# Transposes between the halves of a tile's product, two tiles later, and other banks for the prologue's transposes

## The chip, the core and the metric

The kernel runs on one core of a Trainium2 chip. The core has TensorE (PE; its weight loads, PEld, overlap its matmuls), VectorE (DVE), ScalarE (ACT), GpSimd (POOL) and SyncE (SP), which issues the transfers. Each engine works through its own instructions in order and waits on semaphores for the others. PE writes into PSUM, which has eight banks of 128 x 512 float32 values. The metric is the device time of one execution in microseconds; the kernel before takes 1225.94 us (median of three runs, 1224.2 to 1227.89).

## What is computed

One layer of an encoder over 1024 tokens with 1024 features: a mixer (a gated linear recurrence beside latent attention) and a convolutional GLU network, each behind a normalisation and with a residual.

```python
h = x
h = h + hybrid_mixer(rms_norm(h, ln_mix_g), ...)   # two groups, each normalised, then y @ w_o
h = h + conv_glu_ffn(rms_norm(h, ln_ffn_g), w_up, ffn_conv_w, ffn_conv_b, w_down)
return rms_norm(h, final_norm_g)

def conv_glu_ffn(xn, w_up, ffn_conv_w, ffn_conv_b, w_down):
    u = xn @ w_up
    u = depthwise_conv(u, ffn_conv_w, ffn_conv_b, FFN_CONV_LEFT)
    return (jax.nn.silu(u[..., :D_FF]) * u[..., D_FF:]) @ w_down
```

## The kernel before

**Number format.** Matmul operands are kept as a high and a low part. `split` (lines 60 to 67) writes the high part with a copy (L62, ACT as a rule) and the low part with a subtraction (L67, on DVE or GpSimd). A product takes three matmuls, high by high, high by low and low by high (L70 to L72 in `mm3`, L1076 in `prod`).

**Stage A, the loop over eight token tiles (L1021 to L1045).** For tile i, in the order of the source: `mla_in(i + 1)` transposes the attention part of the next tile into a PSUM tile `psyt` and splits it into `yl` (high on ACT, low on DVE). `mix` then makes the product of tile i with the output weights in two column halves of twelve matmuls, `pso{i}0b` and `pso{i}1b`, and after each half DVE adds it to the residual `hh[i]` (L930). The tile is stored to `hs` by SP (L1026). `tr2` transposes the scaled tile of one tile earlier on PE (L942) and splits it into the operand forms of the next stage: two forms (`B11`, `B21`) for tiles 0 to 3, one (`B22`) for tiles 4 to 7. `norm2(i)` squares the tile on ACT (L935), works out the root on small columns and scales the tile in place on DVE (L937). GpSimd makes sums and differences of tiles in place (`sums_a`, `sums_b`, L955 to L961), and parts of the first weights are split in between.

All PSUM tiles of this loop come from `oneC`, a pool with four buffers of one bank: psyt, two halves, and one tile for each form of `tr2`.

**Stage B, the prologue of the up-projection (L1084 to L1125).** The product with `w_up` is made by a seven-product scheme for 2 x 2 blocks. Its operand forms are `B11`, `B21`, `B22` and the sums `T1` to `T4`; `tr_sum(f, j)` transposes a quarter of one and splits it (ACT, then DVE). `prod(n, j, bank)` is twelve matmuls. The transposes use PSUM banks that no product needs yet: `spare` takes the next of the list `spares` in turn, and banks are taken off the list before products claim them. The first weights are split here too (`W[0, 1]`, its low part on DVE).

**Order.** Both stages stand in one block in which PE, ACT, DVE, GpSimd and SP each keep the order of the source. A second such block begins behind the transposes of `T4`, with `prod(7, 0)` and `prod(3, 0)`. The two blocks are not tied to each other, so instructions of the second may be put ahead of the first one's last. From the second column pair of weights on, the kernel is a regular stream of products, and then the down-projection.

The lines on which the order of banks rests:

```python
def oneC(name):
    return psC.tile([P, 512], F32, tag="one", bufs=4, name=name)

turn, spares = [0], [VH[0], VH[1], GH, T1, S1]

def spare(name):
    turn[0] += 1
    return spares[turn[0] % len(spares)]
```

Of the kernel before, what the change touches and what calls it, by code (L numbers as in the profile page):

```python
# [20 lines left out]
NT = S // P  # L21
# [19 lines left out]
def encoder_layer(ctx, tc, x, w_in, wq, wk, wv, gw, wo, wup, wdn, vec, g_mix, g_ffn, g_fin, g_q, g_kv, tab_t, tab_n, out):  # L41
    nc = tc.nc
    act, dve, pool, pe = nc.scalar, nc.vector, nc.gpsimd, nc.tensor
# [675 lines left out]
    with ExitStack() as apx2:  # L719
# [112 lines left out]
        for t in range(2, NS - 3):  # L832
            h, i = divmod(t, NT)
# [43 lines left out]
        r1 = rsqrt(ssq[:, 0:NT + 2], NT + 2, 1.0 / 512, "r1")  # L877
# [22 lines left out]
    with sbpool("op", side="right") as op:  # L900
# [18 lines left out]
        def halves(ps):  # L919
            return [ps[:, 0:512], ps[:, 512:1024]]  # L920

        def mix(ps, yl, grp, i=None, rr=None):
            for n in range(2):
                mix_mm(ps[n], yl, grp, n)
                if rr is not None:
                    add_to_h(i, ps, rr, (n,))

        def add_to_h(i, ps, rr, parts=(0, 1)):
            for n in parts:
                dve.scalar_tensor_tensor(out=hh[i][:, ts(n, 512)], in0=ps[n], scalar=rr, in1=hh[i][:, ts(n, 512)], op0=ALU.mult, op1=ALU.add)  # L930
# [15 lines left out]
        def tr2(i, one):  # L946
            if i < 4:
                to_form("B11", i, hh[i][:, 0:512], one)
                to_form("B21", i, hh[i][:, 512:1024], one)
            else:  # L950
                to_form("B22", i, hh[i][:, 512:1024], one)
# [6 lines left out]
        def sums_b(i, eng):  # L958
            a, c = hh[i - 4], hh[i]
            eng.tensor_tensor(out=c[:, 512:1024], in0=c[:, 512:1024], in1=a[:, 0:512], op=ALU.subtract)  # L960
            eng.tensor_tensor(out=a[:, 512:1024], in0=a[:, 512:1024], in1=c[:, 512:1024], op=ALU.subtract)  # L961

        def tr_sum(f, j, one):
            src = {"T1": hh[j][:, 0:512], "T2": hh[j + 4][:, 512:1024], "T3": hh[j + 4][:, 0:512], "T4": hh[j][:, 512:1024]}[f]
            to_form(f, j, src, one)
# [24 lines left out]
        yls = {2: yle[2], 3: lru_in(3)}  # L990
        acc = {0: halves(early[0]), 1: halves(early[1])}
        load_wo(4, st4, wo345[:, 1], False)
        for i in range(2, NT):
# [9 lines left out]
            if i == 3:  # L1003
# [3 lines left out]
                r2 = rsqrt(ssq[:, NT + 2:2 * NT], NT - 2, 1.0 / 512, "r2")  # L1007
# [13 lines left out]
        for i in range(NT):  # L1021
            if i + 1 < NT:
                yls[i + 1] = mla_in(i + 1, oneC(f"psyt{i + 1}"))
            acc[i] = [oneC(f"pso{i}{n}b") for n in range(2)]
            mix(acc[i], yls[i], 1, i, r1[:, NT + i:NT + i + 1] if i < 2 else r2[:, i - 2:i - 1])
            nc.sync.dma_start(out=hs[i], in_=hh[i])  # L1026
            if i >= 1:
                tr2(i - 1, oneC)
            norm2(i)
            if i >= 5:  # L1030
                sums_b(i - 1, pool)
            if 4 <= i < NT - 1:
                sums_a(i, pool)
            if i == 0:
                fetch(0)
            if i == 1:
                split(W[0, 0][:, 0], W[0, 0][:, 1], raw[0][0], "act", "pool")
            if i == 2:
                s3 = stp.tile([P, 4, P], F32, tag="st", name="s30")
                combine(0, s3, pool)  # L1040
            if i in (3, 4):
                W[i - 2, 0] = wp.tile([P, 2, NK, P], F32R, tag="w", name=f"w{i - 2}0")
                split(W[i - 2, 0][:, 0], W[i - 2, 0][:, 1], raw[0][i - 3], "act", "pool")
            if i == 5:
                W[3, 0] = wp.tile([P, 2, 4, P], F32R, tag="w", name="w30")  # L1045
                split(W[3, 0][:, 0], W[3, 0][:, 1], s3, "act", "pool")
                fetch(1)
# [8 lines left out]
        S1, T1 = bank("S", "s1"), bank("T", "t0")  # L1056
        VL, VH = [None, None], [None, None]
        for j in range(2):
            VL[j], VH[j] = bank(f"L{j}", f"vl{j}"), bank(f"H{j}", f"vh{j}")
        GL, GH = bank("GL", "gl0"), bank("GH", "gh0")  # L1060
        turn, spares = [0], [VH[0], VH[1], GH, T1, S1]
# [9 lines left out]
    def prod(n, j, ps, new):  # L1071
        z, ko, f = PRODUCTS[n]
        w, b = W[z, j], B[f]
        for k in range(4):
            for l, r, a_, z_ in ((0, 0, new and k == 0, False), (0, 1, False, False), (1, 0, False, k == 3)):
                pe.matmul(ps, w[:, l, ko + k, :], b[:, r, k, :], start=a_, stop=z_, skip_group_check=True)  # L1076
# [6 lines left out]

    W[0, 1] = wo345[:, 1].rearrange("p z (k n) -> p z k n", k=NK)  # L1084
    c0 = stp.tile([P, S], F32, tag="st", name="c0")
    tr_sum("T2", 0, spare)
    prod(1, 0, VL[0], True)
    sums_a(7, dve)
    tr_sum("T2", 1, spare)
    tr_sum("T2", 2, spare)  # L1090
    split(W[0, 1][:, 0], W[0, 1][:, 1], raw[1][0], "act", "dve")
    copy(c0[:, lo], VL[0])
    prod(2, 0, GL, True)
    tr2(7, spare)
    sums_b(7, dve)
    add(GL, GL, c0[:, lo])
# [15 lines left out]
    copy(C11[1], S1)  # L1112
    add(C11[1], VL[1], C11[1])
    prod(6, 0, VL[0], False)
    tr_sum("T1", 3, spare)
    for j in range(3):
        tr_sum("T3", j, spare)
    copy(c0[:, hi], VL[0])
    spares.remove(T1)
    prod(5, 0, T1, True)  # L1120
    tr_sum("T3", 3, spare)
    for j in range(4):
        tr_sum("T4", j, spare)
# [207 lines left out]
    for j in range(1, NPAIR):  # L1331
# [20 lines left out]
        if j == 1:  # L1352
            GH = bank("GH", f"gh{j}")
# [3 lines left out]
        if j > 1:  # L1357
            prod(6, j, vl, False)
            GH = bank("GH", f"gh{j}")
# [56 lines left out]
    for n, (p, q) in enumerate(todo[:-LAST]):  # L1416
# [10 lines left out]
        acc = ys if p in (1, 3, 5) else xs  # L1427
# [99 lines left out]
```

## Time and profile before

| | |
|---|---|
| median of three runs | 1225.94 us (1224.2 to 1227.89) |
| the profiled execution | 1227.5 us, of which the span is 1225.7 us |
| PE busy | 1167.1 us, 95% of the span |
| DVE, ACT, GpSimd busy | 939.6 us (77%), 641.3 us (52%), 260.2 us (21%) |
| chain that ended last | PE 81%, DVE 12%, ACT 2%, DMA 2%, issue 2% |
| mean granted clock of PE | 0.987 of full speed |

Stage A's loop over tiles lies from 504 to 562 us of the span, stage B from 562 to 597 us, and the regular stream begins near 625 us. The granted clock has two levels, 1.2 and 2.4 GHz; a value between 0.5 and 1 for a stretch says which part of it ran at the lower one. In the timeline a row gives the start, the duration, the engine and line, the operation, what it writes and reads with the shapes, and in brackets the idle time of the engine just before it and what ended that.

### The profile page before, as it was taken

Reading aid. Unit: us, or ns where it says so; the run is one execution under the profiler, and the core shown is the slowest. Engines: PE = TensorE matmul, PEld = TensorE weight load, DVE = VectorE, ACT = ScalarE, POOL = GpSimd, SP = SyncE. Lnnn points to the kernel's source line nnn. Section 1 sums busy time; section 2 is a strip of 40 time slices with the busy share of each in tenths; the row PEclk is TensorE's granted clock in tenths of the full one; section 3 lists DMA queues with packets and bytes.
Section 4 is the critical chain, followed back from the end, with each engine's and each line's share of the span. In section 5 each row is a group of like instructions: output and inputs, shape, how many; then the busy total and the mean of one; then the engine's idle time right before and its main releaser. Section 6 shows DMA issues by size and latency. Waiting matters only on the chain.

```text
span 1225.7 us, 15357 instructions
## 1 busy us (share of the span) xinstructions
PE 1167.1 (95%) x5668; PEld 970.8 (79%) x5668; DVE 939.6 (77%) x1386; ACT 641.3 (52%) x1037; POOL 260.2 (21%) x146
## 2 busy tenths in 40 slices
PE   5999986999999999998899999999999999999997
PEld 5987764788888888776778888888888888888885
DVE  5788789877777765478697778787787877887866
ACT  4735565776767764343554445444444454344453
POOL 2214556621212243254010101101010100000000
PEclk8999998999999999999999999999999999999999
DMA  5311101000000133221233232322333258853333
GB/s 211 96 43 44 43 18 35 18 1 1 1 1 1 35 138 121 68 88 51 60 121 107 77 116 96 120 95 78 112 112 121 80 178 304 288 173 119 96 112 120
DMA packets 93579, 113.38 MB, mean 92 GB/s; under 512 B 5184, under 2 KB 59840, under 8 KB 93504
## 3 DMA queue, kind: packets, MB, share of 16 engines
q1 hardware_dynamic: 93504, 112.40, 27.8%
q8 instruction: 44, 0.72, 0.3%
q14 instruction: 31, 0.25, 0.1%
HBM read 82.76 MB, written 28.57 MB: 91 GB/s over the span
## 4 chain that ended last, share of the span: by engine, by line
PE 81%; DVE 12%; ACT 2%; DMA 2%; issue 2%; SPq 0%; DVEq 0%; POOL 0%; ACTq 0%
PE vl L1076 19%; PE x L1269 9%; PE y L1269 7%; PE gh L1076 5%; PE gl L1076 4%; PE pt L763 4%; PE p L1076 4%; PE av L774 3%; PE av L773 2%; PE sc L70 2%; PE sc L71 2%; PE sc L72 2%; DVE bc L223 1%; PE pso L71 1%; PE pso L72 1%
## 5 line engine op out<-in xcount | busy, mean ns | idle before, releaser
L1076 PE MATMUL vl<-T,w 128*128 128x512 f32 x792 | 195.7, 396 | 2.0 <-ACT gl L1082 1.5
L1076 PEld LDWEIGHTS vl<-T,w 128*128 128x128 f32 x792 | 148.5, 188 | 37.8 <-ACT gl L1082 1.9
L67 POOL TENSOR_TENSOR w<-rg,w 128x1024 fp32r<-128x1024 f32 x21 | 52.0, 2475 | 363.8 <-ACT w L62 227.6
L749 DVE TENSOR_REDUCE nm<-sc 128x1 f32<-128x1024 f32 x64 | 78.1, 1221 | 29.9 <-PE sc L72 29.6
L62 ACT ACTIVATE ptb<-pt 128x512 fp32r<-128x512 f32 x128 | 70.2, 596 | 58.3 <-PE pt L763 57.1
L67 DVE TENSOR_TENSOR ptb<-pt,ptb 128x512 fp32r<-128x512 f32 x128 | 83.0, 680 | 7.0 <-ACT ptb L62 7.0
L756 ACT ACTIVATE pr<-sc,nm 128x1024 f32<-128x1024 f32 x64 | 71.7, 1120 | 2.6 <-DVE nm L749 2.6
L763 PE MATMUL pt<-ident,pr 128*128 128x128 f32 x512 | 67.7, 274 | 3.3 <-DVE ptb L67 3.3
L763 PEld LDWEIGHTS pt<-ident,pr 128*128 128x128 f32 x512 | 59.3, 140 | 14.1 <-DVE ptb L67 5.3
L1076 PE MATMUL gh<-B,w 128*128 128x512 f32 x264 | 64.3, 392 | 1.4 <-DVE T L67 1.4
L773 PE MATMUL av<-ptb,vt 128*128 128x256 f32 x256 | 64.9, 292 | 0.0
L1173 ACT ACTIVATE c<-gh,vv 128x512 f32<-128x512 f32 x22 | 17.1, 778 | 89.1 <-DVE gh L1079 89.1
L774 PE MATMUL av<-ptb,vt 128*128 128x256 f32 x256 | 62.6, 283 | 0.0
L1076 PE MATMUL p<-T,w 128*128 128x512 f32 x252 | 62.5, 397 | 0.0
L1269 PE MATMUL x<-abS 128*128 128x512 f32 x264 | 60.2, 389 | 0.0
L1269 PE MATMUL y<-abS 128*128 128x512 f32 x264 | 60.2, 389 | 0.0
L1076 PEld LDWEIGHTS gh<-B,w 128*128 128x128 f32 x264 | 49.5, 188 | 13.0 <-DVE T L67 1.7
L1076 PE MATMUL vl<-B,w 128*128 128x512 f32 x240 | 58.4, 392 | 0.0
L1269 PEld LDWEIGHTS x<-abS 128*128 128x128 f32 x264 | 49.5, 188 | 10.3
L1269 PEld LDWEIGHTS y<-abS 128*128 128x128 f32 x264 | 49.5, 188 | 10.3
L1076 PE MATMUL gl<-B,w 128*128 128x512 f32 x240 | 57.6, 389 | 0.0
L1076 PEld LDWEIGHTS p<-T,w 128*128 128x128 f32 x252 | 47.4, 188 | 11.4
(647 smaller groups left out, 2972.8 us busy)
## 6 DMA issues: line engine op xcount, KB each, us to landing
rg<-in_wup SPq DMA_DIRECT2D x22, 512.0 KB, 4.2
rv<-in_wup SPq DMA_DIRECT2D x22, 512.0 KB, 3.8
S<-c SPq DMA_DIRECT2D x44, 256.0 KB, 2.6
wr<-in_wdn SPq DMA_DIRECT2D x44, 256.0 KB, 5.0
stS<-S SPq DMA_DIRECT2D x44, 256.0 KB, 2.9
A<-c SPq DMA_DIRECT2D x33, 256.0 KB, 2.1
stA<-A SPq DMA_DIRECT2D x33, 256.0 KB, 4.5
wost<-in_wo SPq DMA_DIRECT2D x8, 512.0 KB, 3.8
```

The lines of the kernel that those rows point to most:

```text
L62: act.activation(hi, src, AF.Copy)
L67: (dve if lo_on == "dve" else pool).tensor_tensor(out=lo, in0=src, in1=hi.bitcast(F32), op=ALU.subtract)
L70: pe.matmul(ps, l[0], r[0], start=start, stop=False)
L71: pe.matmul(ps, l[0], r[1], start=False, stop=False)
L72: pe.matmul(ps, l[1], r[0], start=False, stop=stop)
L749: dve.reduce_max(nm[t], sc[t], axis=AX, negate=True)
L756: act.activation(pr[t], sc[t], AF.Exp, bias=nm[t], accum_out=rowsum[:, h, i:i + 1])
L763: pe.transpose(pt[:, ts(c, P)], pr[t][:, ts(4 * kh + c, P)], ident)
L773: pe.matmul(av[:, 0:256], lv, ptb[buf][:, 0, c, :], start=(c == 0), stop=False)
L774: pe.matmul(av[:, 0:256], lv, ptb[buf][:, 1, c, :], start=False, stop=(c == NT - 1))
L1076: pe.matmul(ps, w[:, l, ko + k, :], b[:, r, k, :], start=a_, stop=z_, skip_group_check=True)
L1269: pe.matmul(ps, ab[:, 0, l, ts(j, P)], ab[:, 1, r, :], start=a_, stop=z_, skip_group_check=True)
```

## The change

`mix` takes a function and calls it between its two column halves. In the loop, `tr2` runs there, for the tile two earlier (i - 2) where it ran behind both halves for the tile one earlier. `sums_b` follows one iteration later. `tr2(6)` and `sums_b(6)` move behind the loop, to the start of stage B. In stage B the third quarter of `T2` is transposed behind `prod(2, 0)`, so that its split comes behind the split of the weight `W[0, 1]`. From `prod(6)` on the list of banks is set by hand: the transposes ahead of `prod(5)` leave out its bank `T1`, and the last four use the banks `VH`, not `GH`, which `prod(3)` writes next.

```diff
@@ -919,11 +919,13 @@
-        def mix(ps, yl, grp, i=None, rr=None):
+        def mix(ps, yl, grp, i=None, rr=None, between=None):
             for n in range(2):
                 mix_mm(ps[n], yl, grp, n)
                 if rr is not None:
                     add_to_h(i, ps, rr, (n,))
+                if n == 0 and between is not None:
+                    between()
@@ -1022,13 +1024,12 @@
             if i + 1 < NT:
                 yls[i + 1] = mla_in(i + 1, oneC(f"psyt{i + 1}"))
             acc[i] = [oneC(f"pso{i}{n}b") for n in range(2)]
-            mix(acc[i], yls[i], 1, i, r1[:, NT + i:NT + i + 1] if i < 2 else r2[:, i - 2:i - 1])
+            mix(acc[i], yls[i], 1, i, r1[:, NT + i:NT + i + 1] if i < 2 else r2[:, i - 2:i - 1],
+                (lambda: tr2(i - 2, oneC)) if i >= 2 else None)
             nc.sync.dma_start(out=hs[i], in_=hh[i])
-            if i >= 1:
-                tr2(i - 1, oneC)
             norm2(i)
-            if i >= 5:
-                sums_b(i - 1, pool)
+            if i >= 6:
+                sums_b(i - 2, pool)
             if 4 <= i < NT - 1:
                 sums_a(i, pool)
@@ -1083,14 +1084,16 @@
     c0 = stp.tile([P, S], F32, tag="st", name="c0")
+    tr2(6, spare)
+    sums_b(6, pool)
     tr_sum("T2", 0, spare)
     prod(1, 0, VL[0], True)
     sums_a(7, dve)
     tr_sum("T2", 1, spare)
-    tr_sum("T2", 2, spare)
     split(W[0, 1][:, 0], W[0, 1][:, 1], raw[1][0], "act", "dve")
     copy(c0[:, lo], VL[0])
     prod(2, 0, GL, True)
+    tr_sum("T2", 2, spare)
     tr2(7, spare)
     sums_b(7, dve)
@@ -1112,12 +1115,14 @@
     prod(6, 0, VL[0], False)
+    spares[:] = [VH[0], VH[1], GH]
     tr_sum("T1", 3, spare)
     for j in range(3):
         tr_sum("T3", j, spare)
     copy(c0[:, hi], VL[0])
-    spares.remove(T1)
     prod(5, 0, T1, True)
+    spares[:] = [GH, VH[0], VH[1], VH[0], VH[1]]
+    turn[0] = -1
     tr_sum("T3", 3, spare)
     for j in range(4):
         tr_sum("T4", j, spare)
```

## Rows read from the trace of the kernel before

**Rows 1.** Waits, 505 to 630 us: engine, line, waited for: total us, times, longest

```profile
PE pshB L942 <- DVE h L937: 3.8, 3, 1.6
PE vl L1076 <- DVE wo L67: 2.6, 1, 2.6
PE gh L1076 <- DVE T L67: 1.4, 1, 1.4
PE t L1076 <- DVE T L67: 1.3, 1, 1.3
```

**Rows 2.** Timeline of iterations 1 and 2, the forms, psyt, stores and scaling

```profile
515.78 0.68 DVE L67 TENSOR_TENSOR yl<-psyt,yl 128x512 fp32r<-128x512 f32 x1
...
516.52 0.42 PEld L942 LDWEIGHTS pshB<-ident,h 128*128 128x128 f32 x4 [0.18 <-DVE yl L67]
...
517.18 0.42 PEld L915 LDWEIGHTS psyt<-ident,yn 128*128 128x128 f32 x4 [0.24 <-DVE h L930]
...
522.85 2.21 DVE L937 SCALAR_TENSOR_TENSOR h<-h,rh1r,g 128x1024 f32<-128x1024 f32 x1 [2.78 <-DMA hs<-h]
524.98 0.68 DVE L67 TENSOR_TENSOR yl<-psyt,yl 128x512 fp32r<-128x512 f32 x1
```

**Rows 3.** Timeline of PE in iteration 4, to the start of iteration 5

```profile
533.54 0.60 PE L915 MATMUL psyt<-ident,yn 128*128 128x128 f32 x4
...
536.75 0.39 PE L70 MATMUL pso41b<-wo,yl 128*128 128x512 f32 x1
...
540.35 0.60 PE L915 MATMUL psyt<-ident,yn 128*128 128x128 f32 x4
```

**Rows 4.** Timeline of ACT, DVE and GpSimd in the same iteration

```profile
534.28 1.06 ACT L935 ACTIVATE jk<-h 128x1024 f32<-128x1024 f32 x1
...
536.57 1.28 DVE L937 SCALAR_TENSOR_TENSOR h<-h,rh3r,g 128x1024 f32<-128x1024 f32 x1
...
536.78 3.32 POOL L67 TENSOR_TENSOR w<-rg,w 128x1024 fp32r<-128x1024 f32 x1 [7.86 <-ACT w L62]
...
537.77 0.68 DVE L67 TENSOR_TENSOR yl<-psyt,yl 128x512 fp32r<-128x512 f32 x1
...
539.67 0.75 DVE L930 SCALAR_TENSOR_TENSOR h<-pso41b,r2r,h 128x512 f32<-128x512 f32 x1 [0.56 <-PE pso41b L72]
```

**Rows 5.** The tile hs: its eight stores, issue to landing

```profile
DMA to landing us min/median/max: 2.6/2.8/4.9
```

**Rows 6.** Timeline of PE: two matmul groups behind waits

```profile
200.64 0.50 PE L70 MATMUL psq<-cT,wq1h 128*128 128x512 f32 x1 [3.56 <-POOL wq1h L66]
...
572.35 3.85 PE L1076 MATMUL vl<-B,wo 128*128 128x512 f32 x10 [2.58 <-DVE wo L67]
```

**Rows 7.** Stretches: us, PE, PEld, DVE, ACT, POOL busy (x), PEclk, DMA, GB/s

```profile
200.00:205.00 5.00, 4.36 (x12) 3.36 (x13) 3.86 (x4) 2.44 (x3) 4.62 (x4) 0.66 0.01 3
...
524.00:529.00 5.00, 3.70 (x20) 2.86 (x21) 4.74 (x10) 3.07 (x6) 4.71 (x3) 1.00 0.24 97
...
570.00:575.00 5.00, 2.65 (x8) 2.13 (x9) 4.79 (x7) 0.00 (x0) 0.00 (x0) 0.83 0.01 3
```

**Rows 8.** Timeline of DVE and GpSimd near 551 us; the page's group of GpSimd splits

```profile
551.32 2.20 DVE L937 SCALAR_TENSOR_TENSOR h<-h,rh5r,g 128x1024 f32<-128x1024 f32 x1
...
551.15 1.29 POOL L961 TENSOR_TENSOR h<-h,h 128x512 f32<-128x512 f32 x1
...
L67 POOL TENSOR_TENSOR w<-rg,w 128x1024 fp32r<-128x1024 f32 x21 | 52.0, 2475 | 363.8 <-ACT w L62 227.6
```

**Rows 9.** Timeline: the loop's end (PE, DVE) and the prologue's end (PE)

```profile
559.53 0.39 PE L72 MATMUL pso71b<-wo,yl 128*128 128x512 f32 x1
...
561.80 0.73 DVE L930 SCALAR_TENSOR_TENSOR h<-pso71b,r2r,h 128x512 f32<-128x512 f32 x1
...
594.90 0.60 PE L942 MATMUL gh<-ident,h 128*128 128x128 f32 x4
...
608.79 3.07 PE L1076 MATMUL vl<-T,w 128*128 128x512 f32 x12 [0.47 <-ACT gh L1082]
```

## The prediction

> **What bounds the kernel now.** I read the page first: TensorE (PE) is busy 95% of the span and carries 81% of the chain that ended last, so time can only be won where PE waits. The list of waits from 505 to 630 us was next: in the stretch that the change touches, PE waits 3.8 us for the scaled token tiles (three times), 2.6 us for the low half of a weight split, 1.4 and 1.3 us for PSUM banks that VectorE (DVE) has yet to read [rows 1]. That is 9.1 us, about all the change could remove on PE directly. Then I read the stretch in order of time, because the edit moves work inside a loop that uses only four PSUM banks. Everything behind 625 us is a regular PE stream; a shift of its start is a shift of the end.
>
> **The loop over tiles: who holds which bank.** Each iteration takes five banks in this order: one for the attention transposes of the next tile (psyt), two for the halves of the product, two for the two forms of `tr2`. There are four buffers, so the second form must get the bank of this iteration's psyt, and that bank is free only when DVE has written the low split `yl` of the next tile. The trace shows just that: in iteration 1 the second group of form transposes loads when `yl` has ended (515.78 + 0.68 = 516.46; load at 516.52), and the next psyt loads when a half's add (DVE h L930) has ended, the bank's holder by the same turn [rows 2]. Before the change this costs 0.2 us, since the forms come after both halves. The edit puts them after the first half, 2.7 us earlier in PE's order, and the second half queues behind them.
>
> DVE can't give that bank sooner. Its order is the order of the source: the `yl` split stands behind the scaling of the tile before (L937), and that scaling overwrites the tile which the store `hs` is still reading, so it waits for the store [rows 2]. The new cycle, from the start of one second half to the next, is worked out from these rows: half to its add 2.92 us (536.75 to 539.67), the add 0.75, the store 2.75 (2.6 to 2.8 but for the early ones), the scaling 1.2 until `yl` can start (536.57 to 537.77), `yl` 0.68, four transposes 0.44 and about 0.1 of handover: 8.85 us. PE's own cycle today is 540.35 - 533.54 = 6.8 us [rows 2 to 5]. So PE, which ran through iterations 3 and 4 without a gap, would wait 2.0 us in each of iterations 3, 4 and 5.
>
> **Iteration 2 is worse.** Its second form waits for `yl` of tile 3, which ends at 524.98 + 0.68 = 525.66 in both kernels: it hangs on a slow early store, for which the scaling of tile 1 stands 2.8 us until 522.85, and on 2.21 us of scaling [rows 2], neither touched. PE would have reached it near 519.7, so it stands 6.0 us, in place of 1.6 us now. Second half of tile 2: from 526.2.
>
> **The clock.** After PE idled 3.56 us before 200.64, and 2.58 us before 572.35, the granted clock of the next stretches was 0.66 and 0.83 of full speed, which is a fall from 2.4 to 1.2 GHz for part of them; the ten matmuls at 572.35 took 3.85 us, where 0.23 us apart would give 2.3 [rows 6, 7]. So I put 1.5 us on each wait of 2.6 us or more, and none on waits of 2.0 us (after the 1.6 us wait ahead of 525.2 the clock stayed at 1.00 [rows 7]).
>
> **GpSimd and DVE.** In iteration 3 GpSimd splits a weight (L67) 2.5 us after the square of the tile starts (534.28 to 536.78). Today DVE's scaling began 0.2 us before it, and GpSimd's split took 3.32 us, where such splits take 2.48 on the mean [rows 4, 8]. In the other order DVE pays: the scaling at 551.32 began behind GpSimd's 551.15 and took 2.20 in place of 1.28 [rows 4, 8]. With the forms gone from between, the square starts at once behind the add, so GpSimd is ready 2.5 us after the add, the scaling 2.75 us after it. GpSimd is ahead by 0.2 us, so I take it that the scaling waits out the split: 2.0 us once. PE's wait there becomes 3.4 to 4.0 us, and another 1.5 us of clock follows. The bounds for this term are 0 and 3.5 us.
>
> The Trainium skill, SBUF — State Buffer, "Who interferes with whom", says that a DVE instruction with two SBUF inputs and a GpSimd instruction that reads SBUF exclude each other, and that whoever issues first holds the shared ports for the whole instruction. The two rows above agree with it in both orders. By the rule the term is either the full 2.0 us or nothing, not a share of it.
>
> **Sum of the loop.** From 526.2: +1.5 (clock) and three cycles of 8.85, +2.0 and +1.5 for iteration 3's collision, bring the second half of tile 5 to 557.8; it ends at 560.5. Iterations 6 and 7 have one form each and no such wait: 7.0 (psyt 0.36, 0.6 until the last add frees a bank, halves 2.84 and 2.72, a form 0.44) and 6.0. The last half ends at 573.5, against 559.53 + 0.23 = 559.8 now [rows 9]: **13.7 us later**, or 10.2 without the collision. The waits at 553 and 560 (2.2 us) are gone in that sum already.
>
> **From the loop's end to the matmul that waits for the weight.** Today that is 572.35 - 559.8 = 12.6 us [rows 6, 9]. The wait is for the low split of `W[0, 1]`, fifth in DVE's line behind the last scaling. The edit takes one form's split from ahead of it (T2 of tile 6) and puts another there (B22 of tile 6, by `tr2(6)`): the same count, 0.6 off and 0.6 on. What can be won is DVE's lag: its last add of the loop starts at 561.80, 1.8 us after it could read the half [rows 9]; in the new loop DVE is late by the scaling of tile 6 alone. I take -0.5 us (bounds -1.7 and +0.5), and leave the clock's fall there as it is.
>
> **Banks in the prologue.** After `prod(6)`, T1's bank is left out of the turn: `prod(5)` no longer waits 1.3 us for its last reader. But with three banks, the fourth group of transposes waits for the first one's split: 0.64 + 0.6 + 0.7 = 1.95 us behind its start, where three groups cover 1.3. So 0.7 of the 1.3 is won (bounds 0 and 1.3).
>
> `prod(3)` no longer waits 1.4 us for the bank of the last group. But what follows hangs on that last group (at 594.90), not on `prod(3)`: ScalarE copies out `ts`, splits three weights, a raw tile is fetched and split, and only then comes the copy for which PE waits 0.5 us at 608.79 [rows 9]. The 1.4 us are thus worth 0.4 to the end, from the earlier split alone (bounds: -1.3, if the last two groups go before `prod(7)`, and +2.4, if they go behind `prod(3)`; the order of this seam isn't the order of the source, since today all but one of the matmuls of `prod(7)` run ahead of the last group).
>
> The three terms: -0.5 - 0.7 - 0.4 = -1.6 us.
>
> **Total.** 13.7 - 1.6 = +12.1 us on the profiled execution, whose time of 1227.5 us is 1.8 us over its span. The median of the runs is 1225.94, 1.6 us under that time; the shift is put on the median: **1238.0 us**.
>
> **Rivals.**
> 1. *No collision in iteration 3.* If the store lands before GpSimd's 2.5 us are over, the scaling goes first, as in [rows 4]: 10.2 - 1.6 = +8.6, 1234.5 us. Decided by 0.2 us, hence likely.
> 2. *The seam's last groups go behind `prod(3)`*: 2.8 us more on the chain that ScalarE starts: 1240.8 us (1237.3 without the collision).
> 3. *The other side: the second form's bank is free when PE gets there.* It is if the placement of tiles follows first use rather than a fixed turn, or if `yl` gets ahead of the scaling; it decides where the wait is under 0.7 us an iteration. Then only DVE's own loop counts: store 2.75, scaling 1.2, five reads of PSUM at 0.6 to 0.75, some 7.2 us against 6.8, and the loop ends no later than today, since there too DVE's adds were last. With -1.6, -1.3 and the wait of 1.6 us in iteration 2 gone: 1221 to 1224 us. Against it stand the two handovers of [rows 2], which fit the fixed turn, the first to 0.1 us; and with four banks for five tiles some tile takes psyt's in any order.
> 4. *The edit doesn't do what it says:* the halves hide no wait, because the two-tile delay already removes the wait for the scaled tile, and what is put between the halves only moves. Its price is in the forecast; alone (forms two tiles late, but behind both halves) it would give about -4, 1222.
>
> The Trainium skill, Perfetto Trace Analysis, "Optimization Strategy", takes a gap that repeats on the engine that should be saturated as a sign that the next tile finds no buffer. That speaks against this edit, which would make such a gap of 2.0 us in three iterations; today's rows show only the 0.2 us.
>
> **How the numbers follow.** Forecast 45%; rival 1 28%; rival 2 9%; rivals 3 and 4 together 12%; the rest (a mixture, mostly slower) 6%. A change of 0.3% is 3.7 us, about what a measurement of this kernel can tell from none. Cases one and two and rival 2 are all slower by more; of rivals 3 and 4, half is faster by more and half within. Faster 0.06, within 0.3% 0.08, slower 0.86. The range from 1231 to 1242 takes in the forecast and rivals 1 and 2, with the bounds of the prologue's terms below rival 1 and one more fall of the clock above the rest.
>
> **What would show it.** Right: in the changed profile the list of waits puts PE's form transposes behind the DVE `yl` split, 2 to 4 us in each of iterations 3 to 5 and 6 us in iteration 2; the span between second halves is near 8.9 us; `prod(1)` starts 9 to 13 us later than 562.1; the granted clock falls after tile 2's wait. Wrong: second halves 7 us apart, or form transposes that wait for the scaling alone. If the loop is as said but the end isn't, the error lies in the prologue, and the wait for the weight split, at 2.6 us now, shows how much.

## The result, and the profile after

The kernel after takes **1243.28 us** (median of four executions, 1242.68 to 1243.91), the kernel before beside it 1225.07 us (four, 1223.13 to 1227.89): a ratio of 1.0142, 95% interval 1.0122 to 1.0162. Slower, as forecast, and 1.3 us above the range. The profiled execution of after took 1242.68 us with a span of 1240.9 us, 15.2 us more than the span before; the medians lie 18.2 us apart. The 3 us between these two figures are less than the executions of the kernel before lie apart (4.8 us): its profiled execution, at 1227.5 us, was near the slowest of the four, that of after was the fastest of its four. One execution of each kernel was profiled, and all rows and stretches below come from these.

The list of PE's waits in the kernel after, from 505 to 630 us (engine, tile, line, waited for: total us, times, longest), answers [rows 1]. The lines have moved: L67 is still the low split, L930 (the add) is now L932, L935 (the square) L937, L937 (the scaling) L939, L942 (the form transposes) L944, L1076 (a product) L1077, L1082 (a copy) L1083.

```profile
PE pso21b L70 <- DVE yl L67: 4.0, 1, 4.0
PE vl L1077 <- ACT gh L1083: 3.4, 1, 3.4
PE pso41b L70 <- DVE yl L67: 3.3, 1, 3.3
PE vl L1077 <- DVE wo L67: 3.1, 1, 3.1
PE vl L1077 <- DVE vh L1080: 1.7, 1, 1.7
PE pso31b L70 <- DVE yl L67: 1.2, 1, 1.2
...
PE pso51b L70 <- DVE yl L67: 1.0, 1, 1.0
```

Of the three waits for the scaling (3.8 us) one of 1.2 us is left, now ahead of stage B, and of the two for prologue banks (2.7 us) less than 1 us. Four waits for `yl` (9.5 us) and, at the seam, two of 1.7 and 3.4 us for what DVE and ScalarE do with finished products stand in their place.

The loop of after in the timeline: PE's second halves, then DVE and GpSimd around two of them (start, duration, engine, line, operation, shapes, idle before).

```profile
524.15 0.80 PE L70 MATMUL pso21b<-wo,yl 128*128 128x512 f32 x1 [3.99 <-DVE yl L67]
...
535.13 0.50 PE L70 MATMUL pso31b<-wo,yl 128*128 128x512 f32 x1 [1.18 <-DVE yl L67]
...
545.57 0.50 PE L70 MATMUL pso41b<-wo,yl 128*128 128x512 f32 x1 [3.33 <-DVE yl L67]
...
555.28 0.50 PE L70 MATMUL pso51b<-wo,yl 128*128 128x512 f32 x1 [1.00 <-DVE yl L67]
```

```profile
520.93 2.57 DVE L939 SCALAR_TENSOR_TENSOR h<-h,rh1r,g 128x1024 f32<-128x1024 f32 x1 [1.10 <-DMA hs<-h]
523.42 0.68 DVE L67 TENSOR_TENSOR yl<-psyt,yl 128x512 fp32r<-128x512 f32 x1
...
541.48 2.35 POOL L67 TENSOR_TENSOR w<-rg,w 128x1024 fp32r<-128x1024 f32 x1 [12.79 <-ACT w L62]
...
541.66 3.25 DVE L939 SCALAR_TENSOR_TENSOR h<-h,rh3r,g 128x1024 f32<-128x1024 f32 x1 [0.43 <-DMA hs<-h]
544.83 0.68 DVE L67 TENSOR_TENSOR yl<-psyt,yl 128x512 fp32r<-128x512 f32 x1
```

Each second half starts 0.05 us after a `yl` has ended (523.42 + 0.68 = 524.10, then 524.15; 544.83 + 0.68 = 545.51, then 545.57). It is the half that waits for the bank of psyt, not the second form: the forms come before it in PE's order and run at once. So here the four banks go out in the order in which the tiles are first used, and the fifth user is the half. DVE writes that `yl` behind the scaling, and the scaling of tile 3 takes 3.25 us, since GpSimd's split began 0.18 us ahead of it.

The stretches of after at the waits (us, then PE, PEld, DVE, ACT, POOL busy (x), granted clock, DMA share, GB/s):

```profile
519.00:524.00 5.00, 1.17 (x10) 0.83 (x8) 3.71 (x6) 2.45 (x5) 3.93 (x2) 0.91 0.14 57
524.00:529.00 5.00, 4.85 (x11) 3.80 (x12) 1.95 (x4) 0.00 (x0) 4.46 (x4) 0.50 0.00 0
...
545.00:550.00 5.00, 4.43 (x14) 3.48 (x15) 2.50 (x5) 0.00 (x0) 0.00 (x0) 0.70 0.00 0
```

Behind the 3.99 us wait the granted clock is 0.50, which is 1.2 GHz for the whole of the next 5 us: eleven matmuls where a full clock gives some 22. Before, the stretch from 524 us stood at 1.00 [rows 7].

The seam of after, timeline of PE:

```profile
570.35 0.39 PE L72 MATMUL pso71b<-wo,yl 128*128 128x512 f32 x1
...
583.84 4.04 PE L1077 MATMUL vl<-B,wo 128*128 128x512 f32 x10 [3.13 <-DVE wo L67]
...
605.15 2.46 PE L1077 MATMUL gh<-B,w 128*128 128x512 f32 x10
607.45 1.03 PE L944 MATMUL vh<-ident,h 128*128 128x128 f32 x8
608.24 0.71 PE L1077 MATMUL gh<-B,w 128*128 128x512 f32 x2
610.66 5.83 PE L1077 MATMUL vl<-T,w 128*128 128x512 f32 x24 [1.71 <-DVE vh L1080]
...
622.65 4.37 PE L1077 MATMUL vl<-T,w 128*128 128x512 f32 x12 [3.35 <-ACT gh L1083]
```

The last two groups of transposes (x8 at 607.45) stand behind ten of the twelve matmuls of `prod(3)`. Fifteen us later, at `prod(7, 1)`, PE waits 3.35 us where it waited 0.47 [rows 9], and the twelve matmuls there take 4.37 us in place of 3.07.

To compare kernels I cut the stretch at four rows of PE: the first matmul of `pso10b` (the loop begins), the last matmul of `pso71b` (the loop ends), the ten matmuls of `prod(1, 1)` that wait for `W[0, 1]`, and the first twelve matmuls of `gl` in the regular stream. Each figure is the difference of two starts in the timeline of that kernel.

| kernel | loop | to the weight | seam | sum | against before |
|---|---|---|---|---|---|
| before | 49.34 | 12.82 | 55.00 | 117.16 | |
| after | 60.20 | 13.49 | 58.70 | 132.39 | +15.23 |

These 15.23 us are the whole difference of the spans: 10.9 in the loop, 0.7 up to the weight, 3.7 at the seam. The loop begins at the same place (510.19 and 510.15 us); in the profiled executions of the kernels below it begins between 507.9 and 513.8 us with nothing changed upstream, and such shifts enter the time of an execution too, so the stretches say more of the change than the medians. How far a loop that is left alone strays from one execution to the next, three kernels show: 49.34, 47.91 and 49.08 us.

### The profile page after: what moved, and what is told of

It reads as the page before. It is cut to its first block, busy times and chain, and to the rows that moved or that the text cites. A ratio compares the mean times of both kernels' runs of the same rounds, so it can differ in the third digit from the quotient of the medians.

```text
span 1240.9 us, 15345 instructions
## 1 busy us (share of the span) xinstructions
PE 1173.8 (95%) x5668; PEld 976.2 (79%) x5668; DVE 939.2 (76%) x1386; ACT 641.5 (52%) x1037; POOL 259.8 (21%) x146
## 4 chain that ended last, share of the span: by engine, by line
PE 79%; DVE 14%; DMA 2%; ACT 2%; issue 2%; DVEq 0%; SPq 0%; POOL 0%; ACTq 0%
PE vl L1077 19%; PE x L1274 9%; PE y L1274 7%; PE gh L1077 5%; PE gl L1077 4%; PE pt L763 4%; PE p L1077 4%; PE av L774 3%; PE av L773 3%; PE sc L70 2%; PE sc L71 2%; PE sc L72 2%; DMA hs<-h 1%; DVE bc L223 1%; DVE h L939 1%
## 5 line engine op out<-in xcount | busy, mean ns | idle before, releaser
L1077 PE MATMUL vl<-T,w 128*128 128x512 f32 x792 | 197.1, 398 | 6.8 <-ACT gh L1083 3.4
L1077 PEld LDWEIGHTS vl<-T,w 128*128 128x128 f32 x792 | 149.5, 189 | 43.5 <-ACT gh L1083 3.8
L67 POOL TENSOR_TENSOR w<-rg,w 128x1024 fp32r<-128x1024 f32 x21 | 50.9, 2425 | 370.0 <-ACT w L62 218.7
L67 DVE TENSOR_TENSOR ptb<-pt,ptb 128x512 fp32r<-128x512 f32 x128 | 83.1, 681 | 7.0 <-ACT ptb L62 7.0
L773 PE MATMUL av<-ptb,vt 128*128 128x256 f32 x256 | 66.3, 296 | 0.0
L1077 PE MATMUL gh<-B,w 128*128 128x512 f32 x264 | 64.5, 393 | 0.0
L774 PE MATMUL av<-ptb,vt 128*128 128x256 f32 x256 | 63.9, 287 | 0.0
L1077 PE MATMUL p<-T,w 128*128 128x512 f32 x252 | 62.5, 397 | 0.0
L1077 PEld LDWEIGHTS gh<-B,w 128*128 128x128 f32 x264 | 49.5, 188 | 11.4
L1077 PE MATMUL vl<-B,w 128*128 128x512 f32 x240 | 58.4, 392 | 0.0
L1077 PE MATMUL gl<-B,w 128*128 128x512 f32 x240 | 57.6, 389 | 0.0
L1077 PEld LDWEIGHTS p<-T,w 128*128 128x128 f32 x252 | 47.4, 188 | 11.4
```

The source lines that it names most:

```text
L67: (dve if lo_on == "dve" else pool).tensor_tensor(out=lo, in0=src, in1=hi.bitcast(F32), op=ALU.subtract)
L773: pe.matmul(av[:, 0:256], lv, ptb[buf][:, 0, c, :], start=(c == 0), stop=False)
L774: pe.matmul(av[:, 0:256], lv, ptb[buf][:, 1, c, :], start=False, stop=(c == NT - 1))
```

## The experiments

Theory A is the reading above: the loop is held by psyt's bank, which comes free only with a `yl` behind the scaling and the store; GpSimd's split and the clock add to it; and the new bank lists put the last two groups of transposes behind `prod(3)`, which starts the chain to `prod(7, 1)` late. Each recorded expectation names the rival that its run tells apart. "Seam" and "loop" are the stretches of the table.

**1. The loop without the new bank lists.** The kernel after, with the banks of the prologue taken as before:

```diff
-    spares[:] = [VH[0], VH[1], GH]
     tr_sum("T1", 3, spare)
...
+    spares.remove(T1)
     prod(5, 0, T1, True)
-    spares[:] = [GH, VH[0], VH[1], VH[0], VH[1]]
-    turn[0] = -1
```

> The changed kernel without its last part: behind prod(6) the list of banks is as before, so the transposes use T1 and GH again. Theory A (the loop costs 11.0 us by its end, and the new banks of the prologue's last groups cost another 4.5, because the last two groups now stand behind ten of the twelve matmuls of prod(3)): 1243.3 - 4.5 + 0.8 (the wait for T1 is back) = 1239.5 us. Rival B (all of the loss is the loop's, the banks only win): 1244 us.

Measured: 1237.06 us (1236.1 to 1237.45), ratio 1.0080 [1.0065, 1.0095]; loop 59.53, seam 56.17 us, 2.5 less than in after. Timeline of PE, the last group of transposes and `prod(7, 1)`:

```profile
602.70 0.60 PE L944 MATMUL vh<-ident,h 128*128 128x128 f32 x4
...
617.01 4.59 PE L1077 MATMUL vl<-T,w 128*128 128x512 f32 x12 [2.58 <-ACT gh L1083]
```

The lists cost 2.5 us here, where the expectation has 3.7 (4.5 less 0.8). The rest of the change leaves the seam 1.2 us worse than before, with a wait of 2.58 us and the slow matmuls again; these make up 1.5 us by themselves (4.59 against 3.07).

**2. The new bank lists alone.** The kernel before with after's two lists, the loop untouched.

```diff
+    spares[:] = [VH[0], VH[1], GH]
     tr_sum("T1", 3, spare)
...
-    spares.remove(T1)
     prod(5, 0, T1, True)
+    spares[:] = [GH, VH[0], VH[1], VH[0], VH[1]]
+    turn[0] = -1
```

> The kernel before with only the last part of the change: the two lists of banks behind prod(6) and prod(5). Theory A: the wait for T1 falls by 0.8 us, the last two groups go behind ten matmuls of prod(3) and hold back all that follows, +2.3 to +4.5: 1226.5 to 1229 us. Rival B: both waits for a bank are won, 1223 us.

Measured: 1229.67 us (1227.4 to 1231.84, ten executions), ratio 1.0024 [1.0015, 1.0034]; seam 57.49 us, 2.5 more than before. Timeline of PE:

```profile
591.84 2.47 PE L1076 MATMUL gh<-B,w 128*128 128x512 f32 x10
594.14 1.04 PE L942 MATMUL vh<-ident,h 128*128 128x128 f32 x8
...
607.94 4.61 PE L1076 MATMUL vl<-T,w 128*128 128x512 f32 x12 [1.94 <-ACT gh L1082]
```

The picture of after, in the loop of before: two groups behind ten matmuls of `gh` (`prod(3)`), then a wait at `prod(7, 1)` and slow matmuls. So it is the lists that do it, from either side. Of the 2.5 us, 1.5 are the slow matmuls (4.61 us against 3.07).

**3. Two tiles late, but behind both halves.** The kernel after, `tr2(i - 2)` moved out of the product:

```diff
-            mix(acc[i], ..., (lambda: tr2(i - 2, oneC)) if i >= 2 else None)
+            mix(acc[i], ...)
             nc.sync.dma_start(out=hs[i], in_=hh[i])
+            if i >= 2:
+                tr2(i - 2, oneC)
```

> The changed kernel with the transposes two tiles late, but behind both halves and not between them. Theory A (the loss of the loop is that the second half finds no bank until yl is split): the loop ends where it did before or a little earlier, the seam still costs 4.5: about 1228 us. Rival C (the two tiles of delay cost by themselves, since GpSimd's sums come later): near 1240 us.

Measured: 1230.16 us (1229.77 to 1232.08), ratio 1.0025 [1.0013, 1.0036]; loop 47.07 us, 2.3 less than before, seam 59.86. First halves of tiles 4 to 6, timeline of PE:

```profile
534.23 0.48 PE L70 MATMUL pso40b<-wo,yl 128*128 128x512 f32 x1
...
541.04 0.48 PE L70 MATMUL pso50b<-wo,yl 128*128 128x512 f32 x1
...
547.83 0.48 PE L70 MATMUL pso60b<-wo,yl 128*128 128x512 f32 x1
```

A cycle is 6.8 us, with no wait. The two-tile delay costs nothing in the loop; the place between the halves costs all of the 10.9 us, and 2.3 on top. The scaling of tile 3 still goes before GpSimd's split gets in the way (536.91 and 537.12 us), and takes 1.28 us.

**4. Six banks for the loop.** The kernel after with `bufs=6` in `oneC`.

```diff
-            return psC.tile([P, 512], F32, tag="one", bufs=4, name=name)
+            return psC.tile([P, 512], F32, tag="one", bufs=6, name=name)
```

> The changed kernel with six banks in the loop's pool in place of four (eight are there, four stood idle). Theory A: no half waits for yl, the loop goes at DVE's own cycle of 7.2 us, its end is within 2 us of the kernel before, the seam still costs 4.5: about 1229 us. Rival D (the order of DVE behind the store is the limit, whatever the banks): 1240 us or more.

Measured: 1237.37 us (1234.01 to 1238.38), ratio 1.0079 [1.0061, 1.0096]; loop 51.51 us, 8.7 less than after. No half waits for a bank, but the list of waits still holds `yl`, as the operand of first halves:

```profile
PE pso50b L70 <- DVE yl L67: 2.0, 1, 2.0
...
PE pso30b L70 <- DVE yl L67: 1.1, 1, 1.1
PE pso60b L70 <- DVE yl L67: 1.0, 1, 1.0
```

The bank is 8.7 of the 10.9 us. The 2.2 us left are DVE's order itself: `yl` stands behind a scaling that waits for the store, and the scaling of tile 3 still took 3.30 us beside GpSimd. The time lies between the two that stood, 8 us above theory A's: the loop was 0.2 us over what theory A allows, the seam 4.0 us longer than before, and the profiled execution, at 1238.34 us, also holds a loop that began at 513.81 us, 3.7 us later than in after.

**5. Another bank for the seam.** The kernel after, with `S1` back in the list:

```diff
-    spares[:] = [GH, VH[0], VH[1], VH[0], VH[1]]
+    spares[:] = [S1, VH[0], VH[1], GH, S1]
```

> The changed kernel with other banks for the prologue's last five groups: S1, VH[0], VH[1], GH, S1. S1 is free there, so the fourth group needs no split and the fifth only the first one's. The last group stands behind one matmul of prod(7), and no group behind prod(3). Theory A (the seam costs what the place of the last group in PE's order costs): 2.5 us less from the weight wait to the regular stream than in the changed kernel, and up to 2 more, since the last group comes 2.6 us earlier than in the kernel before: 1238.5 to 1241 us against 1244.5 for the changed kernel on this footing. Rival B (what follows hangs on the fetch of the next raw tile, whenever the group comes): no difference.

Measured: 1235.59 us (1232.53 to 1235.86), ratio 1.0062 [1.0040, 1.0084]; loop 60.40 us as in after, seam 51.91, which is 6.8 us less than after and 3.1 less than before. Timeline of PE:

```profile
602.20 0.66 PE L944 MATMUL s<-ident,h 128*128 128x128 f32 x4
...
617.00 3.06 PE L1077 MATMUL vl<-T,w 128*128 128x512 f32 x12 [0.43 <-ACT gh L1083]
```

The last group comes 5.7 us earlier than the last of after (607.45, its second half from 607.9), the wait is 0.43 us, the matmuls keep their 3.06 us. From the last group to `prod(7, 1)` it is 14.8 us here, 14.3 in run 1 and 13.9 before [rows 9]: nearly the same chain each time, and it starts with that group. By the timelines it runs over ScalarE's splits and copies and a fetch: the raw tile is asked for at 611.96 us in after, at 598.85 before, and ScalarE begins to split it 5.4 and 4.6 us later. The gain was above the expected 2.5 to 4.5 us: `prod(7, 1)` starts 5.5 us earlier, counted from the wait for the weight, and its matmuls are 1.3 us shorter, since the clock's fall went with the wait.

**6. GpSimd's split ahead of the products.** The kernel after; the weight that GpSimd splits in iteration 3 is split before that iteration's products.

```diff
+            if i == 3:
+                W[i - 2, 0] = wp.tile(...)
+                split(W[i - 2, 0][:, 0], W[i - 2, 0][:, 1], raw[0][i - 3], "act", "pool")
             acc[i] = [oneC(f"pso{i}{n}b") for n in range(2)]
...
-            if i in (3, 4):
+            if i == 4:
```

> The changed kernel with the split of W[1, 0] moved ahead of the products of iteration 3, so that GpSimd is done before DVE's scaling of tile 3. Theory A (the scaling waited out GpSimd's split, and PE's longer wait let the clock fall): the scaling of tile 3 takes 1.28 us, not 3.25, iteration 3 to 4 takes 8.9 us, not 10.4, and no fall of the clock in the second half of tile 4: -3.3 us. Rival E (the scaling is slow there for another reason): 3.25 us as before, no gain.

Measured: 1241.22 us (1239.99 to 1242.44), ratio 1.0113 [1.0092, 1.0134]; loop 55.80 us, 4.4 less than after. Timeline of GpSimd, DVE and PE:

```profile
534.09 3.27 POOL L67 TENSOR_TENSOR w<-rg,w 128x1024 fp32r<-128x1024 f32 x1 [3.59 <-ACT w L62]
...
542.30 1.28 DVE L939 SCALAR_TENSOR_TENSOR h<-h,rh3r,g 128x1024 f32<-128x1024 f32 x1 [0.43 <-DMA hs<-h]
...
535.76 0.50 PE L70 MATMUL pso31b<-wo,yl 128*128 128x512 f32 x1 [1.40 <-DVE yl L67]
...
544.24 0.50 PE L70 MATMUL pso41b<-wo,yl 128*128 128x512 f32 x1 [1.37 <-DVE yl L67]
...
552.71 0.50 PE L70 MATMUL pso51b<-wo,yl 128*128 128x512 f32 x1 [1.36 <-DVE yl L67]
```

With the split elsewhere the scaling takes 1.28 us, the cycles are 8.48 and 8.47 us, and no wait is over 1.4 us from tile 3 on. In after these two were 10.44 and 9.71: 1.96 us for the collision, then 1.2 for the clock behind the longer wait. That is 3.2 of the 4.4 us, and 3.3 stood. The other 1.2 are not the split's: behind the same wait as in after (3.98 us, then 3.99) the cycle from tile 2 took 9.81 us, not 10.98. GpSimd pays in its turn (3.27 us behind DVE's scaling of tile 2), where nobody waits for it.

**7. The waits filled with matmuls.** The kernel after with transposes of the identity that nobody reads: 32 between the halves of tile 2, and 24 ahead of `prod(7, 1)`.

```diff
...
+            if i == 2:
+                d = bigC("dummy")
+                for k in range(32):
+                    pe.transpose(d[:, ts(k % 8, P)], ident, ident)
...
+        if j == 1:
+            for k in range(24):
+                pe.transpose(S1[:, ts(k % 4, P)], ident, ident)
         prod(7, j, vl, False)
```

> The changed kernel with 32 more transposes of the identity into an idle bank during PE's wait of iteration 2, and 24 ahead of the second column pair's prod(7). They only keep PE busy. Theory A (the clock falls because PE stands): the second half of tile 2 takes 2.7 us, not 5.3, the prod(7) 3.0, not 4.4: -3.5 to -4 us. Rival F (these matmuls are slow because of what they read): no gain, or a loss of the transposes' time.

Measured: 1238.81 us (1237.19 to 1240.03), ratio 1.0093 [1.0071, 1.0114]; loop 57.99, seam 56.08 us, together 4.8 less than after. Timeline of PE:

```profile
520.18 3.66 PE L1028 MATMUL dummy<-ident 128*128 128x128 f32 x32
524.34 0.50 PE L70 MATMUL pso21b<-wo,yl 128*128 128x512 f32 x1 [0.50 <-DVE yl L67]
...
532.86 0.50 PE L70 MATMUL pso31b<-wo,yl 128*128 128x512 f32 x1 [1.40 <-DVE yl L67]
...
619.45 3.05 PE L1084 MATMUL vl<-T,w 128*128 128x512 f32 x12
```

The half starts when it did in after (524.34 against 524.15), since it waits for the same `yl`; but it runs at full speed, and the next half comes 8.52 us behind it in place of 10.98. So 2.5 us of that cycle were the clock. At the seam the clock was 1.3 us: from `prod(7, 1)` to the next product it is 2.9 us here and 4.2 in after. The other 1.3 us go with a fetch of the raw tile that took 1.35 us less, which the run did not touch. Timeline of ScalarE at the split of that tile, first in after (asked for at 611.96 us), then here (at 609.74):

```profile
617.35 1.06 ACT L62 ACTIVATE w<-rg 128x1024 fp32r<-128x1024 f32 x1 [2.13 <-DMA rg<-in_wup]
...
613.78 1.06 ACT L62 ACTIVATE w<-rg 128x1024 fp32r<-128x1024 f32 x1 [0.78 <-DMA rg<-in_wup]
```

From the request to that split it is 3.9 to 5.7 us in the fourteen kernels. What sets it is not shown.

**8. `yl` ahead of the scaling.** The kernel after; `mla_in` runs one step earlier, so that DVE splits the next tile's attention part before it scales.

```diff
+        yls[1] = mla_in(1, oneC("psyt1"))
         for i in range(NT):
-            if i + 1 < NT:
-                yls[i + 1] = mla_in(i + 1, oneC(f"psyt{i + 1}"))
...
             nc.sync.dma_start(out=hs[i], in_=hh[i])
+            if i + 2 < NT:
+                yls[i + 2] = mla_in(i + 2, oneC(f"psyt{i + 2}"))
             norm2(i)
```

> The changed kernel with mla_in one step earlier: the next tile but one is transposed and split right behind the products, ahead of the scaling, so DVE writes yl before it waits for the store. Theory A (the second half finds no bank because yl stands behind store and scaling in DVE's order): no wait for yl, cycles of 6.8 to 7.2 us, the loop ends as early as in the kernel before or up to 2 us earlier, with the seam's cost left: 1228 to 1230 us. Rival D (four banks are too few for halves and forms in this order, whatever DVE does first): near 1240 us.

Measured: 1231.68 us (1228.5 to 1233.95), ratio 1.0036 [1.0024, 1.0047]; loop 48.19 us, 1.15 less than before and 12 less than after; seam 60.27. The transposes still run between the halves, with four banks, and no half waits. Timeline of DVE and PE:

```profile
536.79 3.31 DVE L939 SCALAR_TENSOR_TENSOR h<-h,rh3r,g 128x1024 f32<-128x1024 f32 x1 [0.42 <-DMA hs<-h]
...
540.82 0.66 PE L915 MATMUL psyt<-ident,yn 128*128 128x128 f32 x4 [1.28 <-DVE h L932]
```

The collision of tile 3 is still there, and costs PE 1.28 us in place of 3.33. So it was DVE's order that made the bank late. The 1228 to 1230 us of theory A were missed by 2: the seam took 1.6 us more than in after, with the same lists.

**9 to 12. The parts put together.** Four kernels on one chip, beside the kernel before (1226.19 us, 22 executions): the loop of before with `T1` out of the turn and the list of run 5; run 3 with that list; run 8 with that list; and the last with the early split of run 6 as well. The edit of the first:

```diff
     prod(6, 0, VL[0], False)
+    spares[:] = [VH[0], VH[1], GH]
...
-    spares.remove(T1)
     prod(5, 0, T1, True)
+    spares[:] = [S1, VH[0], VH[1], GH, S1]
+    turn[0] = -1
```

> The kernel before with banks S1, VH and GH for the last five groups of the prologue's transposes (S1 in the turn), and T1 left out of the turn ahead of prod(5); the loop untouched. Theory A (the gain of the S1 run belongs to the seam and needs nothing of the changed loop): the stretch from the second group of the tile that waits for the weight to the first group of the regular stream is 52 to 53 us, where the kernel before takes 55.0; PE's wait at prod(7, 1) is under 1.4 us; the loop is as before; the whole is 2.0 to 3.0 us faster, about 1222.5. Rival G (the S1 run only had slack there because its loop ended 11 us late, so that weights and raw tiles lay ready): 54.5 to 55.5 us for that stretch, and no change in the whole.

> The kernel after with the transposes two tiles late but behind both halves, and the banks S1, VH and GH at the seam. Theory A: loop and seam add: the loop ends 2.1 us earlier than in the kernel before, the stretch to the regular stream takes 52 us in place of 55.0; 4 to 5 us faster than before, about 1221. Rival G: the seam gives nothing once the loop is on time: 59 to 55 us for that stretch, within 2 us of before.

> The kernel after (transposes between the halves) with the split of the next tile's attention part one step earlier, ahead of the scaling on DVE, and the banks S1, VH and GH at the seam. Theory A: the loop ends 0.4 to 1.2 us earlier than before (one collision at tile 3 left), the stretch to the regular stream takes 52 to 53 us: 2.5 to 4 us faster than before, about 1222. Rival G: 55 to 60 us for that stretch, from the same to 5 us slower.

> As the run with the earlier attention split and the S1 seam, with the weight that GpSimd splits in iteration 3 taken ahead of that iteration's products, so that DVE's scaling doesn't fall beside it. Theory A: the scaling of tile 3 takes 1.3 us in place of 3.3, psyt no longer waits for it, the loop ends 2 to 3 us earlier than before and the whole is 1 to 2 us faster than the run without the early split, about 1220.5. Rival: DVE's adds are the loop's bound there, and the earlier GpSimd split falls beside another DVE instruction with two SBUF inputs: no difference to the run without it, or up to 1 us slower.

| kernel | median us | ratio, 95% interval | loop | to the weight | seam |
|---|---|---|---|---|---|
| before's loop, new seam | 1223.08 | 0.9980 [0.9970, 0.9989] | 49.08 | 12.82 | 50.22 |
| behind both halves, new seam | 1222.44 | 0.9969 [0.9958, 0.9981] | 47.11 | 12.92 | 51.64 |
| `yl` first, new seam | 1224.82 | 0.9984 [0.9975, 0.9994] | 48.29 | 13.52 | 51.47 |
| the same and the early split | 1221.46 | 0.9963 [0.9951, 0.9976] | 46.48 | 13.17 | 51.66 |

The rival of these runs, that the seam's gain needs a late loop, falls: the seam is 50 to 52 us in all four, with a loop that is on time. All four beat the kernel before, the last by 4.7 us, and there the scaling of tile 3 takes its short time (timeline of DVE):

```profile
534.41 1.28 DVE L939 SCALAR_TENSOR_TENSOR h<-h,rh3r,g 128x1024 f32<-128x1024 f32 x1 [0.43 <-DMA hs<-h]
```

The first won more at the seam than expected (50.22, where 52 to 53 stood), in part because its `prod(1, 1)` ran at full speed (1.2 us); of that below. The second won 3.8 us where 4 to 5 stood. The third missed its expectation (2.5 to 4 us faster; 1.4 by the medians), though its stretches came out as expected, 3.9 us less than before together: its profiled execution, at 1222.91 us, was one of its fastest. The early split gave 1.8 us of the loop, and 3.4 us by the medians, where 1 to 2 stood.

## Why the prediction was right and wrong

**Right.** The direction, and the mechanism: one user of the four banks holds psyt's, that bank waits for `yl`, `yl` for the scaling, the scaling for the store. Runs 4 and 8 show the two links apart: more banks take 8.7 us off, DVE's other order 12 us. The collision of tile 3 came, by 0.18 us, and cost 1.96 us where 2.0 stood. The bank of `prod(5)` won 0.8 us (from the first of the four groups to the product 2.42 us, 595.16 to 597.58, where it was 3.20 before), where 0.7 stood.

**Wrong in a link.** "So the second form must get the bank of this iteration's psyt" went by the order of the source. By order of first use it is the second half that gets it, which stands behind the forms in any case. The mechanism is the same, but the forms' transposes no longer stand between `yl` and the half: it starts 0.05 us behind `yl`, where the sum had 0.54 (transposes 0.44, handover 0.1). Rival 3 expected such a placement to free PE; it doesn't, as its own last sentence says, because five tiles in four banks leave no other choice.

**The loop: 13.7 forecast, 10.9 measured.** Three terms of the sum were off.
- The end of iteration 2's wait: the second half of tile 2 began at 524.15 us, 2.05 earlier than the forecast 526.2. Of this, 0.5 is the wrong link; the rest is a `yl` that ended 1.56 us earlier. The prediction called the late store of tile 1 and the scaling behind it "neither touched". Both were: the scaling took 2.57 us, not 2.21, but it stood 1.10 us for the store, not 2.78, and 0.9 to 1.2 us in all eleven kernels whose transposes come two tiles late (after and ten of the runs); 2.4 to 2.8 in the three with the loop of before. What in the loop of before holds the store is not shown.
- The cycle: 8.85 forecast, 8.48 without clock and collision (run 6), three times 0.37 less: 0.5 off for the wrong link, and 0.14 on, since half to add took 3.06 us (535.13 to 538.19 in after) and not 2.92.
- The clock behind the first wait: 1.5 forecast, 2.5 in after (by run 7), since all of the half ran at 1.2 GHz. Behind the same wait of 3.96 to 3.99 us the cycle took 10.98 us in after, 10.08 in run 1, 10.78 in run 5 and 9.81 in run 6, against 8.52 in run 7, so the price was 1.3 to 2.5, and that after paid the most is luck. Behind the collision it was 1.2 where 1.5 stood.

Together -2.05 - 1.1 + 1.0 - 0.3 = -2.5; the loop's last two iterations were another 0.4 us shorter than forecast, which gives about the 2.8 that are missing.

**To the weight: -0.5 forecast, +0.7 measured.** The step took it that DVE would come out of the loop less late. The wait for `W[0, 1]` grew from 2.58 to 3.13 us instead, with as many splits ahead of it. DVE's last add of the loop starts 2.66 us behind the start of PE's last matmul, where it was 2.27. The stretch is longer in every run with `tr2(6)` and `sums_b(6)` behind the loop (12.9 to 13.9 us against 12.8). The step also left out what the edit gives GpSimd to do there. Timeline of GpSimd and DVE in after, then of DVE before:

```profile
577.16 1.29 POOL L962 TENSOR_TENSOR h<-h,h 128x512 f32<-128x512 f32 x1
577.25 2.28 DVE L939 SCALAR_TENSOR_TENSOR h<-h,rh7r,g 128x1024 f32<-128x1024 f32 x1
...
566.75 1.28 DVE L937 SCALAR_TENSOR_TENSOR h<-h,rh7r,g 128x1024 f32<-128x1024 f32 x1
```

One of GpSimd's sums of `sums_b(6)` begins 0.09 us ahead of the scaling of tile 7, behind which the split of `W[0, 1]` stands. That scaling takes 2.27 to 2.29 us in the eleven kernels with `sums_b(6)` behind the loop, 1.28 in the three without. From the last add to that scaling it is 0.7 us less than before, so 0.3 of its 1.0 us is left, beside the 0.4 by which the add is late. The sign was wrong: a second collision of the kind that the prediction priced in iteration 3 came here, 1.0 us that it put at nothing; without it the stretch would be some 0.3 us shorter than before (an estimate from these rows). No run took it out.

**The seam: -1.1 forecast, +3.7 measured. This is the step that failed.** Rival 2 named the mechanism, the last groups behind `prod(3)`, and gave it 9% and 2.8 us. It came true. Run 2 shows it alone at +2.5, run 1 shows its absence at -2.5. Two things were put at nothing or too low. The prediction took it that the two blocks would be merged as before, but the choice of banks decides that order (runs 2 and 5); by what rule the groups on `VH` fall behind `prod(3)` was not tried. And the wait which follows brings the clock down: 4.37 us for twelve matmuls that take 3.06 when the wait is 0.43. Of the 3.7 us, 1.3 are these matmuls, 1.5 the later place of the last group (counted from the wait for the weight), and 0.9 a longer chain behind it, most of it the fetch.

**The sum.** The errors of 2.8 us too much in the loop and of 1.2 and 4.8 too little behind it leave 12.1 forecast against 15.2 in the traces. That these lie so near is luck. Put on the 1225.94 us of before, the 15.2 would be 1241.2, inside the range; the last 2 us up to the median of after lie within what executions of one kernel differ by. With the seam as forecast the time would have been well inside it.

**Rivals.** 1 (no collision) did not occur. 2 occurred, on top of the forecast and not in place of it: forecast and rival 2 together are the 1240.8 us that the prediction put on it, and with the seam's 1.3 us of clock about 1242. That this comes near the measured time is luck again, since the loop's 2.8 us too much are still in it. 3 was right about its remedy (`yl` ahead of the scaling brings the loop to the time of before or under, run 8), wrong that the kernel would get it by itself. 4 had the right ground: the delay alone takes the waits away, and the halves hide nothing. Its price of 4 us was reached only with the seam mended (run 3 with the new list, 3.8 us).

## What to carry over

Before work is put into the middle of a product, count the buffers by order of first use and ask who frees the one that is reused next: here an order on DVE that had cost PE 0.2 us an iteration came to cost 8.5 us a cycle in place of 6.8. Where two blocks meet whose order is kept by hand, look in the timeline where the last instructions of the first one land: one list of banks put two groups of transposes behind a product, another didn't, and 6.8 us lay between them, 1.3 of these by the clock. And price a new wait with its second bill, the slow matmuls that may follow it.

## What the runs showed of the hardware

- **The clock behind a wait at `prod(7, 1)`.** Behind waits of 0.19, 0.43 and 0.47 us its twelve matmuls took 3.06 or 3.07 us; behind 1.94, 2.58, 3.35, 3.42, 3.56 and 3.69 us they took 4.61, 4.59, 4.37, 5.49, 4.57 and 5.49. With the wait filled by transposes they took 3.05. The length of the wait does not order the price; why 3.35 us cost less than 1.94 stays open.
- **The same wait, with and without a fall.** In the kernel before and in the one with only its seam mended, the ten matmuls of `prod(1, 1)` follow the same work and the same 2.58 us. One took 3.85 us [rows 6], the other 2.61, with a granted clock of 1.00 for the stretches from 560 to 590 us. Timeline of PE of that kernel:

```profile
572.75 2.61 PE L1076 MATMUL vl<-B,wo 128*128 128x512 f32 x10 [2.58 <-DVE wo L67]
```

  In run 6 there was none behind 3.13 us either (2.60 us). So a fall behind such a wait seems to be a matter of the execution, though no kernel was profiled twice to show it, and 1.2 us of a difference here need not be the kernel's. Part of the seam of 50.22 us in that kernel is this.
- **GpSimd and DVE.** The scaling of a tile took 1.28 us alone and 3.24 to 3.31 us wherever a GpSimd split had begun just ahead of it; in the other order the split took 3.27 in place of some 2.4 us. The Trainium skill, SBUF — State Buffer, "Who interferes with whom", calls the ports that the two share an exclusive lock. These rows agree to 0.2 us: GpSimd's split ended 2.17 us after the scaling had begun (541.48 + 2.35 = 543.83, and 541.66), and 2.17 + 1.28 = 3.45, where 3.25 was measured. An instruction of DVE on a single column stretched as well: in after, in the root of tile 6, 1.05 us in place of 0.16 (568.10, beside a GpSimd difference that ran from 567.84 to 569.14).
